# Negated scores and GpSimd reciprocals, batched conditioning sums and gains folded into weights in a two-layer hybrid transformer block

## The chip, the cores and the metric

The kernel runs on one core of one Trainium2 chip. Engines are named as in the profile: PE (TensorE), PEld (its weight load), DVE (VectorE), ACT (ScalarE), POOL (GpSimd) and SP (SyncE, which issues the transfers). The metric is the device time of one execution in microseconds (us); lower is better.

## The reference

A block of two layers works on 256 tokens of width 1024. In each layer a vector `c` gives shift, scale and gate of two normed branches: a mixer and a SwiGLU feed-forward part. Cut to what matters here:

```python
def dense_causal_attention(q, k, v, log_decay_cum=None):
    s = einsum('bhqd,bhkd->bhqk', q_i, k) * dk ** -0.5
    if log_decay_cum is not None:
        s = s + F[..., None] - F[:, :, None, :]        # forget gate
    p = softmax(where(kpos <= qpos, s, -inf)); return p @ v

def hybrid_mixer(h, ...):
    q_f,k_f,v_f,f_logit,q_m,k_m,v_m,c_q,c_kv,k_r = split(h @ w_in)
    F = cumsum(log_sigmoid(f_logit + b_forget), axis=1)
    o_f = dense_causal_attention(q_f, k_f, v_f, F)     # 4 heads
    o_m = moba_attention(q_m, k_m, v_m, t5_table)      # 4 heads, T5 bias
    q_lat = rmsnorm(c_q, g_q_lat) @ w_uq               # 8 latent heads
    kv = rmsnorm(c_kv, g_kv_lat) @ w_ukv
    o_c = dense_causal_attention([q_nope, rope(q_rot)], [k_nope, rope(k_r)], v_c)
    return concat(rmsnorm per group of (o_f, o_m, o_c)) @ w_out
```

## The kernel before

A product in full precision is made of three: each weight tile is split into a high part `wh` (ACT, L102) and the rest `wl` (DVE, L103), each activation likewise, and PE multiplies low by high, high by high and high by low (L148 to L150 with the weights stationary, L170 to L172 with the tokens stationary). The weights come through a stream of 512 KB transfers (`raw_*`) on SP's queue, with four raw buffers and six of `wh` and `wl`.

The conditioning is a stream of `w_ada` chunks beside it. Part of the chunks goes over PE (`adap`, L274), the others over DVE, which reduces a 128x1024 tile against the row of `c` (`adaw`, L266). The sums land in `adasum`; two small DVE instructions per chunk then add the bias and apply the gain (`ab`, L294 and L296, for shift and scale; `gcol`, L320 and L321, for gates). These steps wait in a list `todo` and are interleaved with the mixer and the feed-forward part by `fill`.

The attention runs over pairs of heads: four latent pairs, two forget-gate (fox) pairs and two MoBA pairs in each layer, thus 16 softmaxes in a layer and 32 in all. Queries come in two tiles of 128; the first sees 128 keys, the second 256, so a head has scores `s` of 128x384 (L458 and L460). `softmax` adds the bias and finds the maximum on DVE (L433, L435), negates it (`nm`, L438), takes exponentials with their sums `sm` on ACT (L440, L441), the reciprocal `ri` on DVE (L443), and scales both parts of `e` on POOL (L444, L445). PE transposes `e` (`pt`, L451), ACT copies it out (`pts`), and PE forms `o` (L478). For a latent pair the keys are `kx` and the queries `qx`, which DVE makes from the projection `qp` (L761).

A framework schedules each engine's order from the order in which the code is written and from its own costs; the engines then run in order. Three small loads matter below. The T5 bias: a band copied by ACT (L238) is written four times to memory (`scr`) and read back as `mobab`. The forget gate: a row is written to memory (`rowsgk`) and read back on every partition as `gk` (512 KB), of which DVE makes a bias `fb` for each head (L728, L730). The gates go the same way (`rowsgp`, `gp`).

Of the kernel before, what the change touches and what calls it, by code (L numbers as in the profile page):

```python
# [13 lines left out]
P = 128  # L14
# [30 lines left out]
def block_kernel(ctx, tc, A, out):  # L45
# [59 lines left out]
    def prep(key):  # L105
# [14 lines left out]
        for u in range(nh):  # L120
# [8 lines left out]
            # beside the norms of the layer boundary: small pieces, so that a norm waits less  # L129
            pieces = 2 if kind == "gu" and j < HEADF or kind in ("c", "cq") or l and kind in ("b", "vm", "uq", "ukv") else 1  # L130
            n = step // pieces
            for q in range(pieces):
                sl = slice(q * n, (q + 1) * n)
                last["wl"] = split(wh[:, sl], wl[:, sl], raw[:, sl])
# [23 lines left out]
        # the low parts of h arrive last  # L158
# [9 lines left out]
    def mm3t(ps, x, w, start, stop):  # L168
        # tokens stationary
# [22 lines left out]
    POOL.memset(mhalf, -0.5)  # L192
    zf = wk.tile([P, P], F32, tag="kt", bufs=2, name="zf")
# [6 lines left out]
    # the tensor engine's clock is up by the time that the first weights arrive  # L200
# [4 lines left out]
    # silu(c), repeated over 32 columns  # L205
# [8 lines left out]
    # and as a row on every partition  # L214
# [8 lines left out]
    # T5 bias of the causal tile, as a Toeplitz read of the per-distance values  # L223
    mobab = const.tile([P, 4, S], F32, name="mobab")

    def t5_bias():
# [5 lines left out]
        DVE.tensor_copy(trep, tab[:, :, None].to_broadcast([P, 4, 32]))  # L232
# [6 lines left out]
        # a copy for each partition: row p is read from its element 127 - p on  # L239
# [20 lines left out]
    def ada_chunk(l, which, j):  # L260
        raws = loaded.pop((l, which, j), None) or ada_load(l, which, j)
        if on_dve(l, which, j):
            # features on partitions
            sb = wk.tile([P, 2], F32, tag="adasum", bufs=4, name="adasum")
            for u in range(2):
                i = DVE.tensor_tensor_reduce(out=raws[u], in0=raws[u], in1=crow, op0=ALU.mult, op1=ALU.add,  # L266
                                             scale=1.0, scalar=0.0, accum_out=sb[:, u:u + 1])
                if last.get("ffn"):
                    order_after(i, last["wl"])
            return sb  # L270
# [9 lines left out]
    def ada_columns(l, which, j, sb, dst):  # L280
        """sums of a chunk, features on partitions"""
        if on_dve(l, which, j):
            return sb
# [5 lines left out]
        return dst  # L289

    def ada_scale(l, which, AB, kc, sb):
        ab = AB[:, kc, :]
        o = which * 16 + 2 * kc
        DVE.tensor_tensor(ab, ada_columns(l, which, kc, sb, ab), cols[:, l, o:o + 2], op=ALU.add)  # L294
        gcol = 32 + which * 8 + kc
        DVE.scalar_tensor_tensor(ab[:, 1:2], ab[:, 1:2], 1.0, cols[:, l, gcol:gcol + 1],  # L296
                                 op0=ALU.add, op1=ALU.mult)
# [38 lines left out]
    def rstd_of(square):  # L336
        """square(half, sum): mean squares of the two halves of a row"""
# [20 lines left out]
    def diagonal(t):  # L358
        # a product with the diagonal of the row factors transposes and scales
# [34 lines left out]
    def post_norm(y, GP, t, store=False):  # L394
        # y: two PSUM banks of one token tile
# [19 lines left out]
    def rstd_bc(sq, n, name):  # L415
        # sq: squares, features on partitions; every row of the result holds the rstd of each token
# [13 lines left out]
    def softmax(s, b0, b1):  # L430
        e = wk.tile([P, 384], F32, tag="e", bufs=4, name="e")
        mx = wk.tile([P, 2], F32, tag="mx", bufs=4, name="mx")
        DVE.tensor_tensor_reduce(out=e[:, 0:P], in0=s[:, 0:P], in1=b0, op0=ALU.add, op1=ALU.max,  # L433
                                 scale=1.0, scalar=-3.0e38, accum_out=mx[:, 0:1])
        DVE.tensor_tensor_reduce(out=e[:, P:3 * P], in0=s[:, P:3 * P], in1=b1, op0=ALU.add, op1=ALU.max,  # L435
                                 scale=1.0, scalar=-3.0e38, accum_out=mx[:, 1:2])
# [3 lines left out]
        ACT.activation(e[:, 0:P], e[:, 0:P], AF.Exp, bias=nm[:, 0:1], accum_out=sm[:, 0:1])  # L440
# [21 lines left out]
    class Group:  # L462
        """one normed group of heads: o is kept until the group's rms is known"""
# [5 lines left out]
        def add(self, o_, es, v0, v1):  # L469
# [28 lines left out]
    def fproj(ps, w, h):  # L498
        # one unit of 128 columns over all of D
# [4 lines left out]
    def value_weights(l):  # L504
        """weights of the first token-major projection, per chunk (high, low)"""
# [16 lines left out]
    def mixer(l, h, prepare, fill, after):  # L522
# [592 lines left out]
```

## Time and profile before

| | |
|---|---|
| three runs | 677.71, 676.04, 675.55 us (median 676.04) |
| profiled execution, span of its instructions | 675.6 us |
| PE busy | 639.2 us, 95% of the span |
| DVE, ACT, POOL busy | 451.4 us (67%), 366.5 us (54%), 51.3 us (8%) |
| chain that ended last | PE 74%, DVE 9%, DMA 8%, ACT 3%, POOL 2% |

The span goes from the first to the last instruction on the core; no time beside it is listed for that execution, and the runs lie from 0.05 below it to 2.1 us above. A share of busy time is an average over stages: the two feed-forward parts, 182 to 350 and 490 to 650 us, have no idle time of PE at all, and the stages between are other work with other limits. The chain is followed back from the last instruction, at each step to what released it.

### The profile page before, as it was taken

How to read it: one execution, taken by the hardware profiler on the slowest of the kernel's cores; microseconds unless marked ns; L12 is line 12 of the kernel's file. 1: busy time of each engine (PE TensorE's matmuls, PEld its weight loads, DVE VectorE, ACT ScalarE, POOL GpSimd, SP SyncE). 2: the span in 40 equal slices, each digit the busy share in tenths (PEclk: the TensorE clock that was granted, in tenths of full speed). 3: DMA queues.
4: the chain of work that ended last, by engine and by line, in shares of the span. 5: the costliest groups of instructions: out<-in, count | busy, mean ns of one | idle time of the engine just before them, and what ended most of it. 6: DMA issues, size and time to landing. Idle time of an engine off the chain costs nothing.

```text
span 675.6 us, 12108 instructions
## 1 busy us (share of the span) xinstructions
PE 639.2 (95%) x4543; PEld 565.5 (84%) x4543; DVE 451.4 (67%) x969; ACT 366.5 (54%) x758; POOL 51.3 (8%) x90
## 2 busy tenths in 40 slices
PE   8989759999999999999999999899899999999996
PEld 6878647667999999999978988668799999999994
DVE  2458277888777777798658765775878755555543
ACT  5447427768654444444458665786764444444431
POOL 1000021421000000000001010240100000000000
PEclk9999979999999999999999999899999999999999
DMA  9968595886478898898844875551558676555511
GB/s 320 407 227 286 168 322 179 281 289 215 147 245 316 310 328 304 313 337 290 313 139 147 296 230 184 201 182 64 187 195 276 219 236 184 185 181 185 184 62 63
DMA packets 44410, 155.29 MB, mean 230 GB/s; under 512 B 5136, under 2 KB 6464, under 8 KB 44352
## 3 DMA queue, kind: packets, MB, share of 16 engines
q1 hardware_dynamic: 44352, 154.52, 67.4%
q8 instruction: 36, 0.59, 0.3%
q14 instruction: 22, 0.18, 0.1%
HBM read 152.64 MB, written 1.86 MB: 229 GB/s over the span
## 4 chain that ended last, share of the span: by engine, by line
PE 74%; DVE 9%; DMA 8%; ACT 3%; issue 2%; POOL 2%; SPq 1%; DVEq 0%; POOLq 0%; ACTq 0%
PE gu L148 11%; PE gu L149 11%; PE gu L150 11%; PE y L171 8%; PE y L172 8%; PE y L170 8%; DMA adaw<-in_w_ada_dram 4%; DVE wl L103 3%; PE adap L274 2%; PE o L478 2%; DMA scr<-band 2%; ACT wh L102 1%; DMA raw_b<-in_w_b_dram 1%; POOL rs L343 1%; DVE adaw L266 1%
## 5 line engine op out<-in xcount | busy, mean ns | idle before, releaser
L103 DVE TENSOR_TENSOR wl<-raw_gu,wh 128x1024 fp32r<-128x1024 f32 (+1 forms) x100 | 108.5, 1096 | 68.8 <-ACT wh L102 68.5
L102 ACT ACTIVATE wh<-raw_gu 128x1024 fp32r<-128x1024 f32 (+1 forms) x100 | 94.4, 958 | 92.6 <-PE gu L149 64.5
L148 PE MATMUL gu<-h0fL,wh 128*128 128x256 f32 x304 | 86.2, 283 | 0.0
L148 PE MATMUL gu<-h1fL,wh 128*128 128x256 f32 x304 | 86.2, 283 | 0.0
L149 PE MATMUL gu<-h1fH,wh 128*128 128x256 f32 x304 | 86.0, 283 | 0.0
L149 PE MATMUL gu<-h0fH,wh 128*128 128x256 f32 x304 | 86.0, 283 | 0.0
L150 PE MATMUL gu<-h0fH,wl 128*128 128x256 f32 x304 | 86.0, 283 | 0.0
L150 PE MATMUL gu<-h1fH,wl 128*128 128x256 f32 x304 | 86.0, 283 | 0.0
L266 DVE CUSTOM_DVE_ANT_0 adaw<-adaw,crow 128x1024 f32<-128x1024 f32 x64 | 77.7, 1229 | 8.4 <-DMA adaw<-in_w_ada_dram 8.4
L102 ACT ACTIVATE wh<-raw_dn 128x1024 fp32r<-128x1024 f32 x44 | 46.7, 1062 | 56.8 <-issue 34.7
L171 PE MATMUL y<-wh,hid 128*128 128x512 f32 x176 | 69.6, 396 | 0.0
L170 PE MATMUL y<-wh,hid 128*128 128x512 f32 x176 | 69.5, 396 | 0.0
L172 PE MATMUL y<-wl,hid 128*128 128x512 f32 x176 | 69.5, 395 | 0.0
L103 DVE TENSOR_TENSOR wl<-raw_dn,wh 128x1024 fp32r<-128x1024 f32 x44 | 53.7, 1224 | 23.3 <-ACT wh L102 23.1
L149 PEld LDWEIGHTS gu<-h0fH,wh 128*128 128x128 f32 x304 | 58.3, 192 | 0.4
L149 PEld LDWEIGHTS gu<-h1fH,wh 128*128 128x128 f32 x304 | 58.3, 192 | 0.4
L148 PEld LDWEIGHTS gu<-h1fL,wh 128*128 128x128 f32 x304 | 58.2, 192 | 0.4
L148 PEld LDWEIGHTS gu<-h0fL,wh 128*128 128x128 f32 x304 | 58.2, 192 | 0.4
L150 PEld LDWEIGHTS gu<-h1fH,wl 128*128 128x128 f32 x304 | 58.3, 192 | 0.0
L150 PEld LDWEIGHTS gu<-h0fH,wl 128*128 128x128 f32 x304 | 58.3, 192 | 0.0
L343 POOL TENSOR_TENSOR rs<-rs,mhalf 128x1 f32<-128x1 f32 x16 | 11.0, 687 | 439.1 <-DVE rs L342 439.1
L172 PEld LDWEIGHTS y<-wl,hid 128*128 128x128 f32 x176 | 33.0, 188 | 8.0
(331 smaller groups left out, 1483.1 us busy)
## 6 DMA issues: line engine op xcount, KB each, us to landing
adaw<-in_w_ada_dram SPq DMA_DIRECT2D x96, 512.0 KB, 6.6
raw_gu<-in_w_gu_dram SPq DMA_DIRECT2D x88, 512.0 KB, 4.7
raw_dn<-in_w_dn_dram SPq DMA_DIRECT2D x44, 512.0 KB, 4.7
raw_out<-in_w_out_dram SPq DMA_DIRECT2D x16, 512.0 KB, 5.0
raw_b<-in_w_b_dram SPq DMA_DIRECT2D x12, 512.0 KB, 5.7
raw_a<-in_w_a_dram SPq DMA_DIRECT2D x8, 448.0 KB, 10.0
raw_uq<-in_w_uq_dram SPq DMA_DIRECT2D x4, 512.0 KB
raw_vm<-in_w_vm_dram SPq DMA_DIRECT2D x4, 512.0 KB, 5.0
```

Of the source, the lines that this page charges most:

```text
L102: ACT.activation(dst_h, src, AF.Copy)
L103: return DVE.tensor_tensor(dst_l, src, dst_h.bitcast(F32), op=ALU.subtract)
L148: chain(PE.matmul(ps, w[0], x[1], start=start, stop=False))
L149: chain(PE.matmul(ps, w[0], x[0], start=False, stop=False))
L150: chain(PE.matmul(ps, w[1], x[0], start=False, stop=stop))
L170: PE.matmul(ps, x[1], w[0], start=start, stop=False)
L171: PE.matmul(ps, x[0], w[0], start=False, stop=False)
L172: PE.matmul(ps, x[0], w[1], start=False, stop=stop)
L266: i = DVE.tensor_tensor_reduce(out=raws[u], in0=raws[u], in1=crow, op0=ALU.mult, op1=ALU.add, scale=1.0, scalar=0.0, accum_out=sb[:, u:u + 1])
L274: chain(PE.matmul(ps[32 * g:32 * g + 32, :], crep[:, kc, :], raws[kc // 4][:, g * 256:(g + 1) * 256], start=kc < 4, stop=kc >= 4, tile_pos ...
L343: POOL.tensor_tensor(r, r, mhalf, op=ALU.pow)
L478: PE.matmul(o[64 * u:64 * u + 64, lo:lo + P], v[:, u * 64:(u + 1) * 64], ps[u][:, i * P:(i + 1) * P], start=start, stop=stop, tile_positio ...
```

## The change

Four things are changed.

1. Softmax. The scores come out negated: the query scale, the rotation table, the mask, the T5 table and the forget-gate sums change their sign. DVE then finds a minimum `mn`, which ACT uses as the bias of an exponential with scale -1. The negation `nm` is gone, and each exponential needs its own reduction only. The reciprocal becomes a power of -1 on POOL.
2. Conditioning. DVE's sums go straight into their place in `ab` and `gcol`. The bias and the gain are applied once for eight columns of gates, or for eight chunks of shift and scale (except in the first norm of layer 0, where it stays at one chunk).
3. Latent norms. The gains `g_q_lat` and `g_kv_lat` are applied to the weights `uq` and `ukv` in their split. The two latents share one tile `latH`, `latL`, and are split in fewer, larger pieces.
4. Values. The product with the values takes both query tiles in one matmul for the first block of keys: four instructions for a pair of heads instead of six.

```diff
-    def split(dst_h, dst_l, src):
-        ACT.activation(dst_h, src, AF.Copy)
-        return DVE.tensor_tensor(dst_l, src, dst_h.bitcast(F32), op=ALU.subtract)
+    def split(dst_h, dst_l, src, gain=None):
+        if gain is None:
...
+        ACT.activation(dst_h, src, AF.Copy, scale=gain)
+        return DVE.scalar_tensor_tensor(dst_l, src, gain, dst_h.bitcast(F32), op0=ALU.mult, op1=ALU.subtract)
...
+    gains = {"uq": 48, "ukv": 50}
...
-        DVE.tensor_copy(trep, tab[:, :, None].to_broadcast([P, 4, 32]))
+        DVE.tensor_scalar(trep, tab[:, :, None].to_broadcast([P, 4, 32]), -1.0, None, op0=ALU.mult)
...
-            sb = wk.tile([P, 2], F32, tag="adasum", bufs=4, name="adasum")
...
-                                             scale=1.0, scalar=0.0, accum_out=sb[:, u:u + 1])
+                                             scale=1.0, scalar=0.0, accum_out=dst[:, u:u + 1])
...
-        DVE.tensor_tensor(gc, ada_columns(l, which, KC + j, sb, gc), cols[:, l, o:o + 2], op=ALU.add)
-        DVE.tensor_tensor(gc, gc, cols[:, l, o + 8:o + 10], op=ALU.mult)
         if j == 3:
+            o = 59 + which * 16
+            DVE.tensor_tensor(gc, gc, cols[:, l, o:o + 8], op=ALU.add)
+            DVE.tensor_tensor(gc, gc, cols[:, l, o + 8:o + 16], op=ALU.mult)
...
-        ada_scale(l, which, ABs[l, which], kc, ada_chunk(l, which, kc) if sb is None else sb)
+        if sb is not None:
+            ada_scale(l, which, AB, kc, 1)
+        elif kc == KC - 1:
+            ada_scale(l, which, AB, 0, KC)
...
-                                 scale=1.0, scalar=-3.0e38, accum_out=mx[:, 1:2])
-        nm = wk.tile([P, 2], F32, tag="nm", bufs=4, name="nm")
-        DVE.tensor_scalar(nm, mx, -1.0, None, op0=ALU.mult)
+                                 scale=1.0, scalar=3.0e38, accum_out=mn[:, 1:2])
...
-        ACT.activation(e[:, P:3 * P], e[:, P:3 * P], AF.Exp, bias=nm[:, 1:2], accum_out=sm[:, 1:2])
+        ACT.activation(e[:, P:3 * P], e[:, P:3 * P], AF.Exp, bias=mn[:, 1:2], scale=-1.0, accum_out=sm[:, 1:2])
         ri = wk.tile([P, 2], F32, tag="ri", bufs=4, name="ri")
-        DVE.reciprocal(ri, sm)
+        POOL.tensor_tensor(ri, sm, monec, op=ALU.pow)
...
-            for i, (lo, v, start, stop) in enumerate(((0, v0, True, True), (P, v0, True, False), (P, v1, False, True))):
+            for lo, n, v, i in ((0, S, v0, 0), (P, P, v1, 2)):
...
-                ACT.activation(dH, tp[:, sl], AF.Copy, scale=g)
-                DVE.scalar_tensor_tensor(dL, tp[:, sl], g, dH.bitcast(F32), op0=ALU.mult, op1=ALU.subtract)
+            split(latH[:, :, ts_], latL[:, :, ts_], tp[:, :384].rearrange("p (u t) -> p u t", u=3))
...
-            for u in range(2):
-                v = wk.tile([P, S], F32, tag="ov", bufs=2, name="cqv")
-                DVE.tensor_scalar(v, cq[:, u * S:(u + 1) * S], cols[:, l, 48 + u:49 + u], None, op0=ALU.mult)
-                split(cqH[:, u, :], cqL[:, u, :], v)
+            split(cqH, cqL, cq.rearrange("p (u s) -> p u s", u=2))
```

The scheduler places other instructions differently as well. The first place is DVE in layer 0, between the first and the second latent pair (`s` are scores, `fb` the forget-gate bias, `raw_b` a weight of the fox and MoBA projections). Before:

```order
L435 ISA mx 128x1
L438 TENSOR_SCALAR nm<-mx 128x2
L443 RECIPROCAL ri<-sm 128x2 x2
L728 SCALAR_TENSOR_TENSOR fb<-gk,gqs,shp 128x128
L730 SCALAR_TENSOR_TENSOR fb<-gk,gqs,shp 128x256
L103 TENSOR_TENSOR wl<-raw_b,wh 128x1024
L266 ISA adaw,adasum<-adaw,crow 128x1024
L266 ISA adasum 128x1
L761 TENSOR_TENSOR qx<-qp,qt 128x512
L320 TENSOR_TENSOR gcol<-adasum,first 128x2
L266 ISA adaw,adasum<-adaw,crow 128x1024
L266 ISA adasum 128x1
```

Now:

```order
L453 ISA e,mn<-s,shp 128x256
L453 ISA mn 128x1
L739 SCALAR_TENSOR_TENSOR fb<-gk,gqs,shp 128x128
L741 SCALAR_TENSOR_TENSOR fb<-gk,gqs,shp 128x256
L739 SCALAR_TENSOR_TENSOR fb<-gk,gqs,shp 128x128
L741 SCALAR_TENSOR_TENSOR fb<-gk,gqs,shp 128x256
L104 TENSOR_TENSOR wl<-raw_b,wh 128x1024
L772 TENSOR_TENSOR qx<-qp,qt 128x512
L277 ISA adaw,gcol<-adaw,crow 128x1024
```

The biases of two heads stand where those of one stood, the negation and the reciprocals have left, and the conditioning step `adaw` has moved behind `qx`.

The second place is PE at the same time: the value products `o` of the first pair, the scores `s` of the second, and a projection `qkp`. Before:

```order
L478 MATMUL o<-pts,vc 64x128 x5
L149 MATMUL qkp<-h0aH,wh 128x256
L150 MATMUL qkp<-h0aH,wl 128x256
L148 MATMUL qkp<-h0aL,wh 128x256
L149 MATMUL qkp<-h0aH,wh 128x256
L150 MATMUL qkp<-h0aH,wl 128x256
L148 MATMUL qkp<-h0aL,wh 128x256
L458 MATMUL s<-kx,qx 128x128 x2
L460 MATMUL s<-kx,qx 128x256 x2
```

Now:

```order
L157 MATMUL qkp<-h0aL,wh 128x256
L158 MATMUL qkp<-h0aH,wh 128x256
L495 MATMUL o<-pts,vc 64x256
L474 MATMUL s<-kx,qx 128x128 x2
L476 MATMUL s<-kx,qx 128x256 x2
L495 MATMUL o<-pts,vc 64x256
L495 MATMUL o<-pts,vc 64x128 x2
L159 MATMUL qkp<-h0aH,wl 128x256
L157 MATMUL qkp<-h0aL,wh 128x256
L158 MATMUL qkp<-h0aH,wh 128x256
```

The scores of the second pair have moved ahead of most of the value products of the first and of most of the projection.

The third place is a little earlier, in layer 0, where ACT copies the T5 band (`vm` are MoBA values, `kx` keys, `raw_b` a weight) and SP sends it. ACT before:

```order
L102 ACTIVATE wh<-raw_b 128x1024
L576 ACTIVATE vm<-vps 128x256
L102 ACTIVATE wh<-raw_b 128x1024
L705 ACTIVATE kx<-kp 64x512
L238 ACTIVATE band<-tp 128x384
```

ACT now:

```order
L103 ACTIVATE wh<-raw_b 128x1024
L716 ACTIVATE kx<-kp 64x512 x2
L249 ACTIVATE band<-tp 128x384
L590 ACTIVATE vm<-vps 128x256
L103 ACTIVATE wh<-raw_b 128x1024
```

SP before:

```order
L126 DMA raw_b<-in_w_b_dram 128x1024 x4
L126 DMA raw_out<-in_w_out_dram 128x1024
L242 DMA scr<-band 4x32x384 x4
L306 DMA rowsgk<-row 8x128
L126 DMA raw_out<-in_w_out_dram 128x1024
L245 DMA mobab<-scr 128x4x256
L309 DMA gk<-rowsgk 128x1024
```

SP now:

```order
L132 DMA raw_b<-in_w_b_dram 128x1024 x4
L253 DMA scr<-band 4x32x384 x4
L317 DMA rowsgk<-row 8x128
L132 DMA raw_out<-in_w_out_dram 128x1024
L256 DMA mobab<-scr 128x4x256
L320 DMA gk<-rowsgk 128x1024
```

On ACT the band has moved ahead of the copy of `vm` and of a weight split; on SP the transfer of `raw_out` that stood ahead of `scr` has moved behind `gk`.

## Rows read from the trace of the kernel before

**Rows 1.** The page of the profile, part 1: busy time and share by engine.

```profile
PE 639.2 (95%) x4543; PEld 565.5 (84%) x4543; DVE 451.4 (67%) x969; ACT 366.5 (54%) x758; POOL 51.3 (8%) x90
```

**Rows 2.** Busy time by stretch (columns as in the first line).

```profile
core 0: us, PE busy (x) PEld busy (x) DVE busy (x) ACT busy (x) POOL busy (x), PEclk, DMA share, GB/s
81.00:104.00 23.00, 11.50 (x64) 10.26 (x62) 14.81 (x43) 4.54 (x14) 3.77 (x4) 0.78 0.87 300
104.00:145.00 41.00, 40.13 (x319) 27.49 (x317) 33.45 (x129) 30.98 (x95) 15.57 (x24) 1.00 0.77 253
182.00:350.00 168.00, 168.00 (x1175) 157.00 (x1174) 127.31 (x209) 76.30 (x109) 0.55 (x1) 1.00 0.84 292
490.00:650.00 160.00, 160.00 (x1156) 151.27 (x1156) 95.32 (x129) 73.65 (x104) 0.00 (x0) 1.00 0.62 201
```

**Rows 3.** Waits of PE: total, times, longest (us).

```profile
PE s L458 <- DVE qx L761: 10.9, 4, 8.1
...
PE pt L451 <- POOL e L445: 2.8, 3, 2.3
```

**Rows 4.** The chain that ended last, 55 to 101 us: start, length, what.

```profile
67.84 10.26 DMA scr<-band
...
78.59 6.94 DMA gk<-rowsgk
...
87.43 1.14 DVE adaw L266
...
96.76 2.63 POOL e L445
```

**Rows 5.** Timeline of SP's queue: start, us, line, transfer.

```profile
63.70 0.33 SPq L126 DMA_DIRECT2D raw_out<-in_w_out_dram  x1
```

**Rows 6.** Timeline of ACT: start, us, instruction, [idle before <-releaser].

```profile
63.16 0.39 ACT L576 ACTIVATE vm<-vps 128x256 f32<-128x256 f32 x1 [0.75 <-PE vps L172]
...
64.84 0.59 ACT L705 ACTIVATE kx<-kp 64x512 f32<-64x512 f32 x1
65.46 0.49 ACT L238 ACTIVATE band<-tp 128x384 f32<-128x384 f32 x1
...
93.86 1.06 ACT L102 ACTIVATE wh<-raw_out 128x1024 fp32r<-128x1024 f32 x1 [12.76 <-PE qkp L149]
...
96.09 0.50 ACT L441 ACTIVATE e<-e,nm 128x256 f32<-128x256 f32 x1
```

**Rows 7.** Timeline of DVE at the forget-gate bias and beside POOL.

```profile
85.55 0.35 DVE L728 SCALAR_TENSOR_TENSOR fb<-gk,gqs,shp 128x128 f32<-128x128 f32 x1 [9.89 <-DMA gk<-rowsgk]
85.82 0.48 DVE L730 SCALAR_TENSOR_TENSOR fb<-gk,gqs,shp 128x256 f32<-128x256 f32 x1
86.21 1.22 DVE L103 TENSOR_TENSOR wl<-raw_b,wh 128x1024 fp32r<-128x1024 f32 x1
...
96.75 1.22 DVE L266 CUSTOM_DVE_ANT_0 adaw<-adaw,crow 128x1024 f32<-128x1024 f32 x1
```

**Rows 8.** Timeline of PE around the stall.

```profile
79.35 0.87 PE L478 MATMUL o<-pts,vc 128*64 128x128 f32 x10
...
89.23 1.22 PE L458 MATMUL s<-kx,qx 128*128 128x128 f32 x4 [8.11 <-DVE qx L761]
...
93.78 0.28 PE L148 MATMUL kn<-kvL,wh 128*128 128x256 f32 x1
93.90 0.28 PE L149 MATMUL kn<-kvH,wh 128*128 128x256 f32 x1
```

**Rows 9.** POOL's powers before: count, busy us, mean ns, idle before.

```profile
L556 POOL TENSOR_TENSOR r<-r,mhalf 128x2 f32<-128x2 f32 x2 | 1.4, 696 | 13.7 <-DVE r L555 13.7
```

**Rows 10.** Makers and readers of the reciprocals: duration ns min/median/max.

```profile
L443 DVE RECIPROCAL ri<-sm x32: 145/160/167, 74.6 to 451.8; 128x2 f32<-128x2 f32 x32
L444 POOL TENSOR_SCALAR e<-e,ri x32: 364/372/2390, 74.9 to 452.1; 128x128 f32<-128x128 f32 x32
L445 POOL TENSOR_SCALAR e<-e,ri x32: 469/478/2621, 75.2 to 452.8; 128x256 f32<-128x256 f32 x32
```

More of the change, by code (lines that the diff above doesn't have):

```diff
@@ L99, in chain @@
         return i
-    def split(dst_h, dst_l, src):
-        ACT.activation(dst_h, src, AF.Copy)
-        return DVE.tensor_tensor(dst_l, src, dst_h.bitcast(F32), op=ALU.subtract)
+    def split(dst_h, dst_l, src, gain=None):
+        if gain is None:
+            ACT.activation(dst_h, src, AF.Copy)
+            return DVE.tensor_tensor(dst_l, src, dst_h.bitcast(F32), op=ALU.subtract)
+        ACT.activation(dst_h, src, AF.Copy, scale=gain)
+        return DVE.scalar_tensor_tensor(dst_l, src, gain, dst_h.bitcast(F32), op0=ALU.mult, op1=ALU.subtract)
+    gains = {"uq": 48, "ukv": 50}
     def prep(key):
@@ L131, in prep @@
             n = step // pieces
+            gain = gains.get(kind)
+            if gain is not None:
+                gain = cols[:, l, gain + u:gain + u + 1]
             for q in range(pieces):
                 sl = slice(q * n, (q + 1) * n)
-                last["wl"] = split(wh[:, sl], wl[:, sl], raw[:, sl])
+                last["wl"] = split(wh[:, sl], wl[:, sl], raw[:, sl], gain)
             parts.append((wh[:, :step], wl[:, :step]))
@@ L192, in block_kernel @@
     POOL.memset(mhalf, -0.5)
+    monec = const.tile([P, 2], F32, name="monec")
+    POOL.memset(monec, -1.0)
     zf = wk.tile([P, P], F32, tag="kt", bufs=2, name="zf")
@@ L278, in ada_chunk, with ada_columns @@
         return sb
-    def ada_columns(l, which, j, sb, dst):
-        if on_dve(l, which, j):
-            return sb
+    def ada_columns(sb, dst):
+        if sb is None:
+            return
         ps = pm("adac", 256)
@@ L288, in ada_columns, with ada_scale @@
                           axis=mybir.AxisListType.X)
-        return dst
-    def ada_scale(l, which, AB, kc, sb):
-        ab = AB[:, kc, :]
+    def ada_scale(l, which, AB, kc, n):
+        ab = AB[:, kc:kc + n, :]
         o = which * 16 + 2 * kc
-        DVE.tensor_tensor(ab, ada_columns(l, which, kc, sb, ab), cols[:, l, o:o + 2], op=ALU.add)
+        DVE.tensor_tensor(ab, ab, cols[:, l, o:o + 2 * n].rearrange("p (k u) -> p k u", u=2), op=ALU.add)
         gcol = 32 + which * 8 + kc
-        DVE.scalar_tensor_tensor(ab[:, 1:2], ab[:, 1:2], 1.0, cols[:, l, gcol:gcol + 1],
+        DVE.scalar_tensor_tensor(ab[:, :, 1], ab[:, :, 1], 1.0, cols[:, l, gcol:gcol + n],
                                  op0=ALU.add, op1=ALU.mult)
@@ L332, in scale_step @@
             ABs[l, which] = act.tile([P, KC, 2], F32, tag="ab", bufs=3, name=f"ab{l}{which}")
-        ada_scale(l, which, ABs[l, which], kc, ada_chunk(l, which, kc) if sb is None else sb)
+        AB = ABs[l, which]
+        ada_columns(ada_chunk(l, which, kc, AB[:, kc, :]) if sb is None else sb, AB[:, kc, :])
+        if sb is not None:
+            ada_scale(l, which, AB, kc, 1)
+        elif kc == KC - 1:
+            ada_scale(l, which, AB, 0, KC)
     def rstd_of(square):
@@ L431, in softmax @@
         e = wk.tile([P, 384], F32, tag="e", bufs=4, name="e")
[L432 to L435, printed above, removed]
-                                 scale=1.0, scalar=-3.0e38, accum_out=mx[:, 1:2])
-        nm = wk.tile([P, 2], F32, tag="nm", bufs=4, name="nm")
-        DVE.tensor_scalar(nm, mx, -1.0, None, op0=ALU.mult)
+        mn = wk.tile([P, 2], F32, tag="mn", bufs=4, name="mn")
+        DVE.tensor_tensor_reduce(out=e[:, 0:P], in0=s[:, 0:P], in1=b0, op0=ALU.add, op1=ALU.min,
+                                 scale=1.0, scalar=3.0e38, accum_out=mn[:, 0:1])
+        DVE.tensor_tensor_reduce(out=e[:, P:3 * P], in0=s[:, P:3 * P], in1=b1, op0=ALU.add, op1=ALU.min,
+                                 scale=1.0, scalar=3.0e38, accum_out=mn[:, 1:2])
         sm = wk.tile([P, 2], F32, tag="sm", bufs=4, name="sm")
-        ACT.activation(e[:, 0:P], e[:, 0:P], AF.Exp, bias=nm[:, 0:1], accum_out=sm[:, 0:1])
-        ACT.activation(e[:, P:3 * P], e[:, P:3 * P], AF.Exp, bias=nm[:, 1:2], accum_out=sm[:, 1:2])
+        ACT.activation(e[:, 0:P], e[:, 0:P], AF.Exp, bias=mn[:, 0:1], scale=-1.0, accum_out=sm[:, 0:1])
+        ACT.activation(e[:, P:3 * P], e[:, P:3 * P], AF.Exp, bias=mn[:, 1:2], scale=-1.0, accum_out=sm[:, 1:2])
         ri = wk.tile([P, 2], F32, tag="ri", bufs=4, name="ri")
-        DVE.reciprocal(ri, sm)
+        POOL.tensor_tensor(ri, sm, monec, op=ALU.pow)
         POOL.tensor_scalar(e[:, 0:P], e[:, 0:P], ri[:, 0:1], 1.0, op0=ALU.mult, op1=ALU.mult)
@@ L540, in value1 @@
             return ps
-        kvH = act.tile([P, S], F32R, tag="kvH", name="kvH")
-        kvL = act.tile([P, S], F32R, tag="kvL", name="kvL")
-        cqH = act.tile([P, 2, S], F32R, tag="cqH", name="cqH")
-        cqL = act.tile([P, 2, S], F32R, tag="cqL", name="cqL")
+        latH = act.tile([P, 3, S], F32R, tag="latH", name="latH")
+        latL = act.tile([P, 3, S], F32R, tag="latL", name="latL")
+        cqH, cqL = latH[:, 0:2, :], latL[:, 0:2, :]
+        kvH, kvL = latH[:, 2, :], latL[:, 2, :]
         def latent(t, kv, wq):
@@ L625, in qk_out @@
         def qk_out(ps, i):
-            ACT.activation(qk[:, i], ps.rearrange("p (u s) -> p u s", u=2), AF.Copy, scale=1.0 if i % 2 else 0.125)
+            ACT.activation(qk[:, i], ps.rearrange("p (u s) -> p u s", u=2), AF.Copy, scale=1.0 if i % 2 else -0.125)
         open_units = {}
@@ L713, in mixer @@
         ACT.activation(za, za, AF.Ln, bias=1.0)
-        DVE.tensor_scalar(z, z, -1.0, 0.0, op0=ALU.mult, op1=ALU.max)
+        DVE.tensor_scalar(z, z, 0.0, None, op0=ALU.min)
         nl = act.tile([P, 2, 4], F32, tag="nl", name="nl")
-        DVE.tensor_tensor(nl, z, za, op=ALU.add)
+        DVE.tensor_tensor(nl, z, za, op=ALU.subtract)
         gq = pm("gq", 8)
@@ L1001, in _constants @@
     out["k_ones"] = np.ones((P, P), f)
-    out["k_mask"] = np.where(j[None, :] <= P + p[:, None], 0.0, NEG).astype(f)
+    out["k_mask"] = np.where(j[None, :] <= P + p[:, None], 0.0, -NEG).astype(f)
     half = 16
@@ L1008, in _constants @@
     sin2 = np.concatenate([-sin, sin])
-    out["k_qtab"] = (np.concatenate([np.ones((64, S), f), cos2, sin2]) * QSCALE).astype(f)
+    out["k_qtab"] = (np.concatenate([np.ones((64, S), f), cos2, sin2]) * -QSCALE).astype(f)
     out["k_ktab"] = np.concatenate([cos2, sin2]).T.reshape(2, P, 64).transpose(1, 0, 2).reshape(P, P)
```

18 lines of the change are left out of this document (8 added, 10 removed).

## The prediction

> **What bounds the kernel now.** Part 1 of the page comes first: PE is busy 639.2 us of a span of 675.6 [rows 1], so about 36 us of idle PE are all that the other engines can give back by waiting less. The stretches say where they lie. In the two feed-forward parts PE is busy all the time, 168.00 of 168 us and 160.00 of 160; between 104 and 145 us it lacks 0.9 us; between 81 and 104 us it is busy 11.50 of 23 us, at a granted clock of 0.78 [rows 2]. The waits of PE name that hole: `s` waits for DVE's `qx` four times, 10.9 us in all and 8.1 once, while the largest entry for the softmax, `pt` behind POOL's `e`, is 2.8 us in three waits, one of 2.3 [rows 3].
>
> The chain tells why DVE was late. The four `scr` copies of the T5 band end a piece of 10.26 us; behind them on SP's queue stands `gk`, which takes 6.94 us to land; then DVE works through `fb`, a weight split, one `adaw` (1.14) and `qx` [rows 4]. DVE had stood still for 9.89 us with `fb` at its head until 85.55 [rows 7]. `qx` itself needed none of that, but runs in order behind it. PE begins `s` at 89.23 [rows 8]. After that the chain ends in an `e` on POOL, which took 2.63 us from 96.76 to 99.39 [rows 4], where the median one takes 0.478 [rows 10].
>
> **The band and `gk`.** Before, ACT ran `vm` at 63.16, a weight split, one `kx`, and the band at 65.46 [rows 6]. The new order runs both `kx` right after the preceding split and then the band, ahead of `vm` and of the next split. From the start of `vm` to the band's are 2.3 us, of which one `kx` of 0.6 stays [rows 6]: the band comes about 1.7 us earlier. SP's queue held a `raw_out` ahead of `scr` (issued at 63.70 [rows 5]); it now goes behind `gk`. At the 300 GB/s of the stretch from 81 us on [rows 2] its 512 KB are 1.7 us of transfer, but most of it had moved by the time that the band was ready, so I count nothing. `gk` then lands at 83.8 in place of 85.55. Bounds: 85.2 if the band's inputs don't come earlier too, 82.1 if the transfer counts in full.
>
> **DVE behind `gk`.** Before, from 85.55 to `s` at 89.23 are 3.68 us. Now two heads' `fb` stand there (one costs 0.27 + 0.39 by the starts of the rows [rows 7]): +0.66. The `adaw` has moved behind `qx`: -1.14. So 3.20 us, and `s` begins at 87.0, 2.2 us earlier.
>
> **What PE gets of it.** PE's order has changed against this gain: most of the first pair's `o` and some ten `qkp` records now stand behind `s`. Before, they ran from 79.35 until the wait began at 81.12 (89.23 less 8.11) [rows 8], so, with two records more at 0.12 us each, 2.0 us of work that used to lie ahead of the wait. The wait thus starts 2.0 us earlier and is as long as before, the clock falls as before, and PE reaches the end of the second pair's projections only some 0.2 us earlier. The gain has to come from the next step, the softmax of that pair. Before, all four exponentials stood behind the split of `raw_out` at 93.86, and the last began at 96.09 [rows 6]; then the slow `e` held PE until 99.39. Now the first head's two stand ahead of that split and only the second head's behind it: split from 93.6, two exponentials of 0.4 to 0.5 us each until 95.5, reciprocal 0.8, two scalings of 0.37 and 0.48 at their medians [rows 10], so `e` is ready at 97.1 and the next `s` follows 2.3 us earlier than before. If the `adaw` behind the third `qx` begins first, it costs its 1.14 us. I take -2.0, with bounds of +0.5 (`gk` at 85.2 and `e` held up as before) and -4.5 (`gk` at 82.1, `e` not held up).
>
> **Reciprocals on POOL.** 32 of 0.160 us leave DVE [rows 10], and 32 powers come to POOL. The same operation in the same shape, 128x2, takes 0.696 there [rows 9]. That is +0.54 us on the way from sum to `e`. Against it, the negation, an instruction of the reciprocal's size, is gone, the first exponential no longer waits for the second reduction, and the reciprocal no longer queues on DVE behind 1.22 us instructions. POOL's work grows by 32 x 0.70, 22 us, on 51.3 [rows 1]; between 104 and 145 us it was busy 15.57 of 41 [rows 2], and 12 powers there add 8.4, so it does not become the bound. PE's waits behind POOL outside the stall are below 1 us, so I take 0. Bounds: -1.5 if all those waits and the delays behind them go, +3.5 if one in five of the 0.54 us reaches PE.
>
> What can spoil it is in one row: the `e` of 2.63 us began with an `adaw` on DVE at 96.75 and ended when the second of two had ended [rows 4, 7], so POOL stood still while DVE read two operands from SBUF. The Trainium skill, page "SBUF — State Buffer", section "SBUF: two separate sides", says that such a DVE instruction and a GpSimd instruction that reads SBUF take a shared pair of ports as an exclusive lock, for the whole instruction. The trace agrees (2.63 us against a median of 0.478). By that rule the power, which reads two small tiles, may wait like `e`, where a reciprocal on DVE could not. What such waits would cost is the second rival below.
>
> **Values.** Before, a pair took 12 records of 128 columns, 0.067 us apart (ten in 0.87, the last one long 0.27 [rows 8]): 0.80. Now four of 256 columns and four of 128: with 0.12 between records of 256 columns (93.78, 93.90 [rows 8]), 0.75. For 16 pairs -0.9. Bounds 0 (waits for `pts` absorb it) and -2.0 (the larger ones take 0.1).
>
> **Conditioning and latents.** Some 80 small DVE instructions go (order counts 858 rows before, 712 now, 64 of the difference being negations and reciprocals). Nearly all lie beside matmuls: PE waits for nothing from DVE in the feed-forward parts [rows 2]. They count 0; without that cover they would be some 80 x 0.16, 13 us of DVE, at the reciprocal's price [rows 10]. No row has a split with a gain. The nearest is `fb`, of the same operation: four times the 0.39 us of its 256 columns are 1.56, against the 1.14 to 1.22 of a plain split [rows 7], so three such splits ahead of the mixer would cost up to 1.0; two small multiplications and their separate splits go against it. I take 0, as the plain split's row is nearer in size, with bounds of -0.5 and +1.0.
>
> **Layer 1.** The other three waits for `qx` are 2.8 us [rows 3]. Two negations and two reciprocals less, at 0.16 each, give up to 0.6 per pair where `qx` stands behind them: I take -0.5, bounds -1.5 and +1.
>
> **Sum.** -2.0 - 0.9 - 0.5 = -3.4, on a span of 675.6: 672.2. The median of the runs is 0.4 above the span, so 672.6.
>
> **Rivals.** *Moved, not shortened (0.23).* The stall ends as PE's order lets it, `e` is held by the `adaw` as before, and the value products hide in waits: 675 to 676. For it: PE's projections end only 0.2 us earlier. Against it: half of the exponentials no longer stand behind the split.
>
> *Slower through POOL (0.17).* Each softmax gets +0.54, and powers are held by DVE's 1.14 to 1.22 us instructions in the stretches with many heads. 12 softmaxes lie between 104 and 140 us, 10 between 433 and 452. If ten of the 32 pass on 0.54, the gain of the forecast is halved and more (5.4 against 3.4, +2.0); with one full `adaw` more (1.2) the kernel is at about 679. It decides from about six on. Against it: PE's wait for `pt` in the dense stretch is small, as PE lacks only 0.9 us there [rows 2].
>
> *More (0.08).* `gk` at 82.1 and no hold-up of `e`, -4.5 in the stall, -2 by the values, -1 in layer 1: 668.5.
>
> The forecast holds 0.52. A measurement here can tell 0.3%, 2.0 us, from no change. Faster by more than that: the forecast and "more", 0.60; same 0.23; slower 0.17. The forecast's own range is 670 to 674. The range for 8 in 10 reaches to 668 below and to 678.5 above, into the slower case.
>
> **What would show it.** The band should start near 63.7, `gk` land near 83.8, and `s` of the second pair begin near 87 after a wait of about 8 us; the next `s` near 97.5. `ri` on POOL should have a median of 0.70. If `gk` doesn't land earlier, the first step is wrong; if `s` is earlier and the later one is not, POOL or the order of PE took it. If `pt` waits behind POOL for more than 6 us in all, the second rival is true. If the feed-forward parts change by more than 1 us, I have missed something there.

## The result and the profile after

The changed kernel takes 683.6 us (median of 4 runs, 680.89 to 685.41), against 675.79 for the kernel before in the same comparison. The ratio is 1.0098, with a 95% interval of 1.0074 to 1.0122: slower by about 1%, 7.8 us by the medians and 6.6 by the ratio. The forecast of 672.6 and its range to 678.5 are both missed, on the other side. The profiled execution of the changed kernel took 680.89 us with a span of 678.8, so 2.1 us lie beside the span. It is the fastest of the four, so the two profiles show only 3.2 us of the difference (678.8 against 675.6).

The page's first part, to be read against [rows 1]:

```profile
PE 638.4 (94%) x4479; PEld 560.1 (83%) x4479; DVE 438.5 (65%) x832; ACT 364.3 (54%) x753; POOL 81.2 (12%) x123
```

PE's work is the same to 0.8 us, DVE has lost 13 us and POOL has gained 30. The same stretches as in [rows 2], with the same columns:

```profile
81.00:104.00 23.00, 15.34 (x100) 13.30 (x101) 15.00 (x37) 8.50 (x24) 6.92 (x9) 0.85 0.82 309
104.00:145.00 41.00, 34.91 (x251) 21.69 (x250) 29.80 (x87) 27.48 (x86) 25.80 (x34) 0.96 0.77 263
182.00:350.00 168.00, 168.00 (x1186) 157.50 (x1185) 124.92 (x179) 76.25 (x108) 0.00 (x0) 1.00 0.86 295
490.00:650.00 160.00, 160.00 (x1155) 151.01 (x1154) 95.19 (x125) 74.94 (x111) 0.00 (x0) 1.00 0.62 204
```

The feed-forward parts have not moved. The hole between 81 and 104 us is smaller: PE is busy 15.34 us there in place of 11.50. The gap has opened behind it: from 104 to 145 us PE does 34.91 us in place of 40.13, and POOL 25.80 in place of 15.57. The waits of PE, to be read against [rows 3]:

```profile
PE pt L467 <- POOL e L460: 7.9, 7, 2.2
PE s L474 <- DVE qx L772: 7.4, 2, 6.5
...
PE pt L467 <- POOL e L461: 2.4, 3, 1.1
```

The wait for `qx` has lost 3.5 us in all. The one for POOL's two scalings of `e` is 10.3 us in ten waits; before it was the 2.8 of [rows 3] and these 1.3 for the first scaling:

```profile
PE pt L451 <- POOL e L444: 1.3, 2, 1.1
```

Where it lies is in PE's timeline:

```profile
86.38 1.22 PE L474 MATMUL s<-kx,qx 128*128 128x128 f32 x4 [6.48 <-DVE qx L772]
...
97.83 0.90 PE L467 MATMUL pt<-first,e 128*128 128x128 f32 x3 [2.16 <-POOL e L460]
98.56 0.61 PE L474 MATMUL s<-kx,qx 128*128 128x128 f32 x4
...
108.27 0.33 PE L467 MATMUL pt<-first,e 128*128 128x128 f32 x1 [1.48 <-POOL e L460]
...
109.69 0.44 PE L467 MATMUL pt<-first,e 128*128 128x128 f32 x2 [0.97 <-POOL e L461]
...
113.04 0.71 PE L474 MATMUL s<-kx,qx 128*128 128x128 f32 x4
```

The third and the fourth pair's scores in the kernel before:

```profile
99.91 0.64 PE L458 MATMUL s<-kx,qx 128*128 128x128 f32 x2
...
112.72 0.61 PE L458 MATMUL s<-kx,qx 128*128 128x128 f32 x4
```

The second pair's scores begin at 86.38 (89.23 in [rows 8]) and the third pair's at 98.56 (99.91 before). By then 2.9 and 1.4 us are won. Then the transposes wait at 108.27 and 109.69, and the fourth pair's scores come 0.3 us later than in the kernel before.

POOL's part of it, the power and the two scalings, to be read against [rows 9, 10]:

```profile
L459 POOL TENSOR_TENSOR ri<-sm,monec x32: 692/701/1720, 74.7 to 454.7; 128x2 f32<-128x2 f32 x32
L460 POOL TENSOR_SCALAR e<-e,ri x32: 374/493/1454, 75.5 to 455.5; 128x128 f32<-128x128 f32 x32
L461 POOL TENSOR_SCALAR e<-e,ri x32: 476/482/1692, 75.9 to 455.9; 128x256 f32<-128x256 f32 x32
```

### The profile page after: what moved, and what is told of

The parts are those of the page before. It is cut to its first block, busy times and chain, and to the rows that moved or that the text cites. A ratio compares the mean times of both kernels' runs of the same rounds, so it can differ in the third digit from the quotient of the medians.

```text
span 678.8 us, 11875 instructions
## 1 busy us (share of the span) xinstructions
PE 638.4 (94%) x4479; PEld 560.1 (83%) x4479; DVE 438.5 (65%) x832; ACT 364.3 (54%) x753; POOL 81.2 (12%) x123
## 4 chain that ended last, share of the span: by engine, by line
PE 68%; POOL 9%; issue 8%; DVE 5%; DMA 5%; ACT 4%; SPq 1%; POOLq 0%; DVEq 0%; ACTq 0%
PE gu L157 11%; PE gu L158 11%; PE gu L159 11%; PE y L181 7%; PE y L179 7%; PE y L180 7%; POOL ri L459 3%; POOL e L461 2%; POOL e L460 2%; DMA adaw<-in_w_ada_dram 2%; DVE wl L104 2%; DMA scr<-band 1%; PE o L495 1%; PE adap L285 1%; POOL rs L360 1%
## 5 line engine op out<-in xcount | busy, mean ns | idle before, releaser
L459 POOL TENSOR_TENSOR ri<-sm,monec 128x2 f32<-128x2 f32 x32 | 27.9, 872 | 135.9 <-ACT e L457 128.0
```

The costliest lines, as they stand in the source:

```text
L459: POOL.tensor_tensor(ri, sm, monec, op=ALU.pow)
```

## The experiments

All times are medians of runs on the same chip as runs of the kernel before, whose medians lay at 676.5 to 676.9 us in these; no run of the changed kernel stands beside them, its 683.6 us is the result above. The ratio to the kernel before has its 95% interval behind it. Differences of some 1.5 us between two kernels with 4 to 12 runs each are at the edge of what can be told.

**The reciprocal on DVE, in the changed kernel.**

```diff
-        POOL.tensor_tensor(ri, sm, monec, op=ALU.pow)
+        DVE.reciprocal(ri, sm)
```

> The changed kernel with the reciprocal back on DVE (all else of the change stays). Theory A (POOL: a power and two scalings per softmax, 0.80 + 0.83 us, one softmax of a pair behind the other, hold up the transposes): PE's waits for pt behind POOL fall from 10.3 us to below 4, and the time to 669 to 674 us, below the kernel before. Theory B (the other order on PE and DVE costs the time, not the power): 680 us or more, waits for pt about as they are. Either way the wait for the forget-gate row stays, the second pair's scores near 86.5 us.

678.03 us, 1.0017 (0.9994 to 1.004). Undoing the power alone gives back 5.6 us. PE's waits for `pt` behind POOL fall to 4.1 us, as theory A has it, but the time lies between the ranges of the two theories. The rest of the change, which the prediction had at -3.4, is thus worth +1, which can't be told from nothing.

**The power alone, in the kernel before.** The same line the other way.

> The kernel before with only the reciprocal moved to POOL as a power of -1. Theory A: 680 to 684 us, slower by 4 to 8, with PE's waits behind POOL's e from 4 to over 8 us. Theory B: within 2 us of the kernel before.

687.57 us, 1.0179 (1.0142 to 1.0215): 10.9 us slower than the kernel before, more than theory A's 4 to 8 and far from theory B's 2, with 13.3 us of waits for `pt` behind POOL. The power costs the time both ways. Whether by its own length or by the order isn't told here, since the scheduler places rows of PE, DVE and ACT differently in this kernel too; for that there are the idle powers below.

**The old value products**, in the changed kernel, and with the reciprocal on DVE.

```diff
-            for lo, n, v, i in ((0, S, v0, 0), (P, P, v1, 2)):
+            for i, (lo, v, start, stop) in enumerate(((0, v0, True, True), (P, v0, True, False), (P, v1, False, True))):
```

> The changed kernel with the value products as before, six matmuls for a pair. If the predicted 0.06 us per pair is real and on the path: 0.9 us slower than the changed kernel. If the value products hide in the waits behind POOL: within 0.5 us of it.

> As e1_recip_dve, and the value products as before. By the prediction's term it is 0.9 us (0 to 2.0) slower than e1_recip_dve; if the larger matmuls gain nothing, the same within 0.5 us. Theory A has it at 670 to 675 us, theory B at 680 or more.

681.74 us, 1.0079 (1.0053 to 1.0105), and 678.78, 1.0036 (1.0016 to 1.0057): 1.9 below the changed kernel and 0.75 above the one with DVE's reciprocal, where 0.9 above was forecast for both. The sign changes and the intervals overlap, so the merged products are worth nothing that shows here.

**The old conditioning, and the old latents**, each with DVE's reciprocal. The edits put the old functions back (`ada_chunk` to `scale_step`; `gain = None` and the split of the latents by pieces).

> The reciprocal on DVE and the conditioning steps as before (bias and gain per chunk). If the batching costs nothing and gains nothing, as the prediction has it: within 1 us of e1_recip_dve (678.0). If the other placement that follows from it is what ate the expected gain of the rest of the change: 674 us or less.

> The reciprocal on DVE and the latents as before (gains on the latents, small splits). e1_recip_dve shows PE waiting 1.2 us for latL in layer 1 and the first scores of layer 1 about 2 us later than in the kernel before. If the larger latent splits are the cause: 675.5 to 676.5 us, 1.5 to 2.5 below e1_recip_dve, and no wait for latL. If not: within 1 us of it.

674.44 us, 0.9961 (0.9943 to 0.9979), and 675.07, 0.997 (0.9956 to 0.9984). Each alone is faster than the kernel with both of the new parts (678.03) by 3 to 3.6 us. With the old latents PE's wait of 1.2 us for `latL` in layer 1 is gone. Both undone at once:

> The reciprocal on DVE, conditioning and latents as before: of the change only the negated scores (no nm, exponentials that wait for their own half) and the merged value products are left. The prediction gives these two some -1.5 us on the kernel before: 674 to 676. If the gains of undoing the conditioning and of undoing the latents add up, 671 to 672.

674.27 us, 0.9975 (0.9959 to 0.9991). The two do not add up: either, or both, gives the same.

**The forget-gate biases behind the third `qx`**, with DVE's reciprocal, and in the kernel before.

```diff
-            DVE.tensor_tensor(qx, qp.rearrange("p (u s) -> p u s", u=2),
+            last["qx", l, hp] = DVE.tensor_tensor(qx, qp.rearrange("p (u s) -> p u s", u=2),
...
+            for i in (i0, i1):
+                order_after(i, last["qx", l, 2])
             return fb
```

> The reciprocal on DVE, and the forget-gate biases ordered behind the third latent pair's qx, so that no instruction ahead of the second qx waits for gk. If DVE's wait for gk is what makes the stall of 6.5 us: the second pair's scores come near 82 us in place of 86.2, and the kernel is 3 to 5 us faster than e1_recip_dve (673 to 675). If the stall only moves to the conditioning tiles that DVE needs next: within 1 us of e1_recip_dve.

> The kernel before with the same order for the forget-gate biases and nothing else. If the wait for gk is worth its 8.1 us of PE's idle time less what the conditioning tiles hold up: 671 to 673 us, faster than the kernel before by 3 to 5. If the stall moves: within 1 us of it.

670.01 us, 0.9896 (0.9872 to 0.992), and 668.5, 0.9877 (0.9856 to 0.9898): 8.0 us below the kernel with DVE's reciprocal and 8.4 below the kernel before, where 3 to 5 were expected. In the first of the two, ACT's order is the same as without the constraint and PE's differs by a few score records, so DVE's wait for `gk` is shown to make the stall. Part of it moves, as its timelines of PE and of DVE show:

```profile
79.05 0.71 PE L474 MATMUL s<-kx,qx 128*128 128x128 f32 x4
...
89.89 0.58 PE L157 MATMUL qp<-latL,wh 128*128 128x256 f32 x1 [5.29 <-DVE mn L453]
```

```profile
86.90 1.23 DVE L277 CUSTOM_DVE_ANT_0 adaw<-adaw,crow 128x1024 f32<-128x1024 f32 x1 [8.22 <-DMA adaw<-in_w_ada_dram]
```

The second pair's scores come at 79.05. Then DVE stands still for 8.22 us with a conditioning tile at its head, which stands ahead of that pair's reductions, and PE waits 5.29 us behind these.

**The negated scores and the merged products**, with the biases late; and the merged products alone.

> As e11_negation_and_values, with the forget-gate biases behind the third qx. If the two parts that are left are worth anything: below e9_before_fb_late (668.5), 666 to 668. If not: within 1 us of it.

> The kernel before with the forget-gate biases behind the third qx and the merged value products. By the term of the prediction 0.9 us (0 to 2.0) below e9_before_fb_late: 667.6.

671.1 us, 0.9921 (0.9906 to 0.9935), and 668.17, 0.9872 (0.9857 to 0.9888). The merged products gain 0.3 us, which is nothing, and the negated scores lose 2.9 us, though 32 instructions have left DVE; neither of the two expectations had a loss.

**The joint wait put back.** 32 copies of the minima, which both exponentials read:

```diff
+        DVE.tensor_scalar(nm, mn, 1.0, None, op0=ALU.mult)
...
-        ACT.activation(e[:, 0:P], e[:, 0:P], AF.Exp, bias=mn[:, 0:1], scale=-1.0, accum_out=sm[:, 0:1])
+        ACT.activation(e[:, 0:P], e[:, 0:P], AF.Exp, bias=nm[:, 0:1], scale=-1.0, accum_out=sm[:, 0:1])
```

> e12_negation_values_fb_late (671.1 us) with 32 DVE copies of the two minima, which both exponentials read, so that both wait for both reductions as in the kernel before. Its order is that of e13_before_fb_late_values row for row, the copy in the place of the negation. If taking the negation out cost 3 us by letting the scheduler put weight splits between the two exponentials of a softmax: 667 to 669 us, with 32 instructions more on DVE than e12. If the negated scores cost by something else: 670 to 672.

667.6 us, 0.9866 (0.985 to 0.9881): 3.5 us faster than without the copies, and level with the merged products alone, whose order it has. ACT's timeline without the copies, then with them:

```profile
102.86 0.39 ACT L449 ACTIVATE e<-e,mn 128x128 f32<-128x128 f32 x1
...
103.25 1.04 ACT L103 ACTIVATE wh<-raw_out 128x1024 fp32r<-128x1024 f32 x1
...
109.94 0.60 ACT L636 ACTIVATE qk<-qkp 128x512 f32<-128x512 f32 x1 [5.00 <-PE qkp L159]
...
110.59 0.49 ACT L450 ACTIVATE e<-e,mn 128x256 f32<-128x256 f32 x1
```

```profile
101.50 3.91 ACT L103 ACTIVATE wh<-raw_out 128x1024 fp32r<-128x1024 f32 x4 [0.85 <-PE qkp L158]
...
107.24 0.39 ACT L451 ACTIVATE e<-e,nm 128x128 f32<-128x128 f32 x1
...
107.62 0.49 ACT L452 ACTIVATE e<-e,nm 128x256 f32<-128x256 f32 x1
```

Without the joint wait the second exponential of one softmax stands 7.7 us behind the first (102.86, 110.59), with a weight split and a `qk` between them, and the `qk` waits 5.00 us for PE. With it, the weight splits go first and the two follow each other. In the other two pairings of the joint wait it does not help:

> e1_recip_dve with the joint wait of both exponentials (32 DVE copies of the minima). If the split halves cost the same 3 us here as between e12 and e16: 674 to 676 us. If the order that the conditioning and the latents make is what holds e1_recip_dve at 678: within 1.5 us of it.

> e8_dve_recip_fb_late (670.0 us) with the joint wait. It differs from e16_halves_joined (667.6) by the batched conditioning and the gains in the weights alone. If these two are worth nothing by themselves: 667 to 668.5. If they cost by the order they make: 669 to 671.

677.94 us, 1.0024 (1.0004 to 1.0044), level with the reciprocal alone on DVE (678.03), and 672.99, 0.9953 (0.9931 to 0.9974), 3 us slower than without the copies (670.01) and slower than either expectation. The last one differs from the 667.6 only by the conditioning and the gains: 5.4 us, in this order.

**Idle powers.** The result is read by nobody; the scalings use DVE's reciprocal. First behind the scalings, then ahead of them, then ahead of them in the kernel before. The edit shown is the first one's; in the other two the power has no such constraint, and POOL runs it ahead of the scalings in their traces.

```diff
+        rj = wk.tile([P, 2], F32, tag="rj", bufs=4, name="rj")
+        order_after(POOL.tensor_tensor(rj, sm, monec, op=ALU.pow), i)
```

> e1_recip_dve with an idle power on POOL behind the two scalings of each softmax, whose result nobody reads; PE, DVE and ACT keep e1_recip_dve's order row for row. If what costs is POOL's queue (the second softmax of a pair waits until the first one's power and scalings are through): 680 to 683 us, most of the 5.5 us between e1_recip_dve and the changed kernel. If it is the longer way of each softmax by itself (0.54 us from sum to scaling): within 1.5 us of e1_recip_dve (678.0).

> e1_recip_dve with an idle power on POOL ahead of the two scalings of each softmax (they still use DVE's reciprocal); PE, DVE and ACT keep e1_recip_dve's order row for row. If the power's 0.7 us and more between the sums and the scalings is what costs: 681 to 684 us, near the changed kernel (683.6). If it is the other order that the scheduler makes for a kernel with the reciprocal on POOL: within 1.5 us of e1_recip_dve (678.0).

> The kernel before with the same idle power ahead of the scalings; its order on PE, DVE, ACT and SP is that of the kernel before, row for row. If the power's time costs: 681 to 687 us, like e2_before_pow (687.6). If the order: within 2 us of the kernel before (676.5).

677.48 us, 1.001 (0.9995 to 1.0025): my first account, POOL's queue, falls for this order, since 32 powers more in it cost nothing where no scaling of their own softmax waits for them. Ahead of the scalings: 679.17, 1.0038 (1.0023 to 1.0052), 1.1 us above the kernel without, near the edge of what can be told. By its expectation that speaks for the order and not for the power's length: in this order the power costs little at either place. The queue was not tried in the order of the kernel before. In the kernel before: 684.46, 1.0089 (1.0058 to 1.0121): 7.8 us above the median of before, 6.0 by the ratio. There the order of PE, DVE, ACT and SP is that of the kernel before, row for row, so the time comes from the power itself. PE's waits for `pt` in that run are twice those before:

```profile
PE pt L455 <- POOL e L446: 5.3, 6, 2.5
...
PE pt L455 <- POOL e L447: 3.0, 4, 1.2
```

Not all of this time is waiting. Over the profiled execution PE is busy 643.0 us for the same 4543 records (639.2 before), 3.8 of the 7.1 us by which the span is longer. The granted clock goes with it; between 104 and 145 us it was 1.00 before [rows 2], and here:

```profile
104.00:145.00 41.00, 38.30 (x294) 27.14 (x294) 31.21 (x124) 28.41 (x88) 26.54 (x36) 0.96 0.77 242
```

Over the nine runs, too: 677.17 us at a mean clock of 0.989, 680.29 and 681.36 at 0.987, and 684.13 to 686.65 at 0.98 to 0.984, where the kernel before runs at some 0.988. So in the three runs at about that clock the power costs 0.5 to 4.7 us, and the rest of the 6 to 8 goes with the lower clock; whether the added waits bring it down was not tried by itself.

## Why the prediction was wrong

**The band, `gk` and `fb`: near in size, in part by luck.** The band started at 64.91, not 63.7: 0.55 us earlier than before, not 1.7. But `gk` itself took 5.19 us to land and not 6.94 [rows 4], and the two misses cancel. One `raw_out` less stands ahead of `scr`, for which the forecast had counted nothing; whether that made `gk` quicker was not separated. The chain of the changed kernel, then its timelines of DVE and of ACT:

```profile
67.27 10.05 DMA scr<-band
...
77.89 5.19 DMA gk<-rowsgk
```

```profile
83.18 0.35 DVE L739 SCALAR_TENSOR_TENSOR fb<-gk,gqs,shp 128x128 f32<-128x128 f32 x1 [8.67 <-DMA gk<-rowsgk]
...
85.64 0.68 DVE L772 TENSOR_TENSOR qx<-qp,qt 128x512 f32<-128x512 f32 x1
```

```profile
64.91 0.49 ACT L249 ACTIVATE band<-tp 128x384 f32<-128x384 f32 x1
...
101.78 0.40 ACT L456 ACTIVATE e<-e,mn 128x128 f32<-128x128 f32 x1 [0.71 <-DVE mn L451]
102.08 0.19 ACT L456 ACTIVATION_READ_ACCUMULATOR e<-e,mn 128x1 f32 x1
102.83 2.96 ACT L103 ACTIVATE wh<-raw_out 128x1024 fp32r<-128x1024 f32 x3 [0.56 <-PE qkp L158]
105.69 0.50 ACT L457 ACTIVATE e<-e,mn 128x256 f32<-128x256 f32 x1
```

`gk` had landed at 83.18 (83.8 forecast), and the 3.20 us from there to `s` came as forecast: `s` began at 86.38 (87.0). The wait was 6.48 us, not as long as before. The third `s` came at 98.56 (97.5), 1.4 us earlier than before where the term had 2.0.

**The step that failed first: "PE's waits behind POOL outside the stall are below 1 us, so I take 0".** The term stood at 0 with an upper bound of +3.5; undoing the power alone gives back 5.6 us. The power's size was right, 0.701 us at the median against 0.70. What was wrong is that small waits before meant slack. The idle powers show that each softmax's own way from sums to `e` counts in the kernel before: +6 to +8 us from the power alone, with the clock's part in it. In the order of the changed kernel the same idle power costs 1.1 us, within the term's bounds, and the other 4.5 go with the order that the power brings, for which the term had nothing. The second rival had the mechanism and its price per softmax, but a chance of 0.17; its sign, over 6 us of `pt` behind POOL, came with 10.3, and its time of about 679 was still 4.6 short.

The row on which that rival rested shows again, with more POOL instructions to be held. POOL and DVE in the changed kernel, near the end of the first mixer:

```profile
132.46 0.73 POOL L459 TENSOR_TENSOR ri<-sm,monec 128x2 f32<-128x2 f32 x1 [0.55 <-ACT e L457]
133.29 1.45 POOL L460 TENSOR_SCALAR e<-e,ri 128x128 f32<-128x128 f32 x1
134.72 1.69 POOL L461 TENSOR_SCALAR e<-e,ri 128x256 f32<-128x256 f32 x1
136.38 1.66 POOL L459 TENSOR_TENSOR ri<-sm,monec 128x2 f32<-128x2 f32 x1
138.14 1.06 POOL L460 TENSOR_SCALAR e<-e,ri 128x128 f32<-128x128 f32 x1
139.19 1.46 POOL L461 TENSOR_SCALAR e<-e,ri 128x256 f32<-128x256 f32 x1
```

```profile
133.02 1.21 DVE L277 CUSTOM_DVE_ANT_0 adaw<-adaw,crow 128x1024 f32<-128x1024 f32 x1
...
134.94 1.21 DVE L277 CUSTOM_DVE_ANT_0 adaw<-adaw,crow 128x1024 f32<-128x1024 f32 x1
...
136.08 1.40 DVE L277 CUSTOM_DVE_ANT_0 adaw<-adaw,crow 128x1024 f32<-128x1024 f32 x1
...
137.76 1.21 DVE L277 CUSTOM_DVE_ANT_0 adaw<-adaw,crow 128x1024 f32<-128x1024 f32 x1
...
139.07 1.23 DVE L277 CUSTOM_DVE_ANT_0 adaw<-adaw,crow 128x1024 f32<-128x1024 f32 x1
```

The scalings, 0.37 and 0.48 alone, take 1.06 to 1.69 here and one of the two powers 1.66, while `adaw` follows `adaw` on DVE. ACT's last sum of the last softmax, and PE's transposes of its `e`:

```profile
133.39 0.19 ACT L457 ACTIVATION_READ_ACCUMULATOR e<-e,mn 128x1 f32 x1
```

```profile
139.26 0.33 PE L467 MATMUL pt<-first,e 128*128 128x128 f32 x1 [1.41 <-POOL e L460]
...
140.70 0.44 PE L467 MATMUL pt<-first,e 128*128 128x128 f32 x2 [1.11 <-POOL e L461]
```

The sums were there at 133.58 and the `e` at 140.65, 7.1 us later, and PE waits 1.41 and 1.11 us for its two parts. Of the 7.1 us, 2.8 passed behind the other head's scalings in POOL's queue (until 136.38). That it is the shared ports that hold POOL fits what the Trainium skill says in "SBUF — State Buffer", section "SBUF: two separate sides", on a DVE instruction with two SBUF inputs against a GpSimd one that reads SBUF; the trace agrees (1.45 to 1.69 against 0.37 and 0.48), but no run here took the conflict away by itself. Over all 32, the power's mean is 0.872 against its median of 0.701 (its busy time of 27.9 us by 32), so being held is some 5.5 us of POOL's time.

**The rest of the power's price goes with the order.** The real power costs the kernel before 10.9 us and the idle one ahead of the scalings 7.8; in the changed kernel 5.6 against 1.1. The remaining 3 to 4.5 us go with the other placement that the scheduler makes for a reciprocal on POOL, since only that and DVE's 32 reciprocals differ. Which moved row costs how much was not separated.

**The second step that failed: a sum of parts, -3.4 for the rest.** It was +1 (-0.4 to +2.7 by the interval). The term for the stall was nearly right up to the third pair. It was given back by placement, and the profiles tell some of the places. From the first scores of the first mixer to the first product of the feed-forward part (worked out from the starts in PE's timeline; us). Each row is one execution; the changed kernel's is the fastest of its four runs (680.89) and that with DVE's reciprocal the slowest of its twelve (680.87), so these two compare places and not totals:

| kernel | pair 1 to 2 | 2 to 4 | 4 to end | sum |
|---|---|---|---|---|
| before | 17.8 | 23.5 | 51.7 | 93.0 |
| changed | 14.2 | 26.7 | 53.9 | 94.8 |
| changed, DVE reciprocal | 14.3 | 26.3 | 52.3 | 92.9 |
| before, idle power ahead | 16.8 | 24.8 | 54.8 | 96.4 |
| negation, values, biases late | 7.7 | 32.3 | 50.2 | 90.2 |
| the same, joint wait | 7.7 | 29.1 | 50.0 | 86.8 |

With DVE's reciprocal 3.5 us are won up to the second pair and 2.8 of them lost by the fourth. In the changed kernel ACT's rows above show one way: an exponential at 101.78, three weight splits of 2.96 us in all, and only then its other half at 105.69; PE's wait at 108.27 follows from it. The prediction counted "the first exponential no longer waits for the second reduction" as a gain; the scheduler used that freedom to put other work between the halves. The joint wait is shown to be worth 3.5 us in one setting, and worth nothing or -3 in two others, so it is no rule. Another place is in the run with the idle power behind the scalings:

```profile
132.67 1.92 PE L497 MATMUL o<-pts,vf 128*64 128x256 f32 x8 [1.91 <-ACT pts L471]
```

Here PE waits 1.91 us for `pts`, which stands on ACT behind two more softmaxes; the run with DVE's reciprocal has the same wait. With the old conditioning PE has none above 0.2 us there, and the kernel is 3.6 us faster. The prediction gave the small DVE instructions 0, since most lie beside matmuls. In the feed-forward parts that stands, where PE is as full as before; that taking them away moves nothing else was wrong. Why each of the edits loses what it does in each order stays open.

**The value products.** -0.9 forecast, -0.3 measured with the biases late, and of both signs elsewhere. The records became fewer and the columns stayed, and a pair's products, in the second mixer before and now, take the same time:

```profile
418.23 0.88 PE L478 MATMUL o<-pts,vc 128*64 128x128 f32 x12
```

```profile
419.76 0.87 PE L495 MATMUL o<-pts,vc 128*64 128x256 f32 x8
```

The forecast's gain of 0.05 us a pair (0.80 less 0.75, a sum of spacings) is not there.

**Layer 1.** -0.5 forecast. From the second set of transposes to the feed-forward part it took 114.5 us before and 115.3 now, and 110.7 to 117.4 in the experiments that have the conditioning and the gains as changed. The term is not to be seen in that spread, and no step of it was separated.

## What to carry to other kernels

A short wait for an engine doesn't say that it has slack: put the added time ahead of its result, with everything else in its order, and see what comes out (here 6 to 8 us from 0.7 us in 32 places in one order, about 1 in another). Moving a 0.16 us instruction to an engine that needs 0.70 for it lengthens each step behind it, and more so where that engine's instructions stretch beside another's, as the scalings did here from 0.37 and 0.48 to 1.06 to 1.69. Where a scheduler sets the order, an edit is judged by the order it makes: parts worth nothing by themselves moved this kernel by 3 us either way, and one ordering constraint on a bias that waited for a transfer was worth 8 us (668.5, and 667.6 with the negated scores, the joint wait and the merged products), more than all of the change.

## What was not expected of the hardware

The time of one kernel varied more than the three runs of before show: 673.77 to 681.89 us over 23 runs, and 677.17 to 686.65 for the one with the idle power. The granted clock goes with it: in the four runs of the changed kernel 0.989 at 680.89 us, 0.98 and 0.979 at 682.54 and 684.65, and 0.975 at 685.41. In the kernel before the records show 0.50, the lower of the two levels, between 88 and 92 us, where the wait of 8.11 us ends (89.23); a wait of 1.33 us ahead of the fourth pair's scores of the second mixer goes with a mean of 0.94 between 424 and 452 us in one experiment (the reciprocal on DVE) and with 1.00 in another (the old conditioning as well).
